# Interleaving two arrays: seven tiles with three shared load buffers in place of eight tiles with four

## The chip, the cores and the metric

The kernel runs on one NeuronCore of a Trainium2 chip. What counts is the device time of one execution in microseconds (us), the median of several runs. A profile was taken of one execution; its span is the time from the first to the last thing that the profiler recorded on that core.

The parts of the core that matter here are 16 DMA engines, which move rows between HBM (the large memory outside the core) and SBUF (128 partitions of memory on the core), VectorE (DVE), which copies inside SBUF, and the two engines that issue DMA transfers, SyncE (SP) and ScalarE (ACT). SP and ACT each have a queue of their own to the 16 DMA engines. Transfers in one queue are taken in order.

## The reference

Two arrays of 32 x 256 x 1024 float32, 33.55 MB each, are woven into one of twice the length: even elements from `x`, odd elements from `y`.

```python
result = np.zeros((batch, seq, dim * 2), dtype=np.float32)
result[..., 0::2] = x
result[..., 1::2] = y
```

No arithmetic is done. 67.1 MB are read and 67.1 MB written.

## The kernel before

`x` and `y` are taken as flat arrays and cut into n = 8 tiles of 128 x 8192 elements: a tile's row on one partition is 8192 elements, 32 KiB, contiguous in HBM. The output of a tile is 128 rows of 16,384 elements. It is made and stored in two halves, h = 0 and h = 1, each 128 x 8192.

There are six SBUF buffers of 32 KiB per partition: `xt` twice and `yt` twice, which tile k uses by k % 2, and `ot` twice, used by half: `ot[0]` always holds the first half of a tile's output and `ot[1]` the second.

Each engine has its own program, and semaphores tie them together:
- **SP** issues the loads. The first half of x(0) comes first (L37), then, in a loop over the tiles, x(k) (L45) and y(k) (L48). From k = 2 on, each load first waits until the tile two before has been copied out of its buffer: the semaphore `woven` counts the copies, four a tile, and the third of tile k-2 is the last that reads its x, the fourth the last that reads its y.
- **ACT** issues the second half of x(0) (L38) and then all stores (L68), two a tile, each after the second copy of its half.
- **VectorE** does four copies a tile, in the order x half 0, y half 0, x half 1, y half 1 (L60 for x, L63 for y). Each writes every second element of `ot[h]`. It waits for the load of x or y at the first half, and before the x copy of each half for the store that had used `ot[h]` in the tile before (`osem[h]`).

At the end ACT waits for the last first-half store, clears the semaphores, and SP waits for the last second-half store. `tile_interleave_kernel` moves the first DMA of SP and the first of ACT to the opening of the program, ahead of a barrier.

In what follows x(k), y(k) are the loads of tile k, and tiles are counted from 0.

Of the kernel before, what the change touches and what calls it, by code (L numbers as in the profile page):

```python
# [3 lines left out]


def _interleave(nc, x, y, out):
    P = 128
    W = 8192
    H = W // 2  # L10

    total = 1
    for s in x.shape:
        total *= s
    n = total // (P * W)
    assert n * P * W == total

    def rows(ap, names, k):
        flat = ap.rearrange("b s d -> (b s d)")
        return flat[k * names : (k + 1) * names].rearrange("(p w) -> p w", p=P)  # L20

    fp32 = mybir.dt.float32
    xt = [nc.alloc_sbuf_tensor(f"xt{b}", [P, W], fp32).ap() for b in (0, 1)]
    yt = [nc.alloc_sbuf_tensor(f"yt{b}", [P, W], fp32).ap() for b in (0, 1)]
    ot = [nc.alloc_sbuf_tensor(f"ot{b}", [P, W], fp32).ap() for b in (0, 1)]

    xsem = [nc.alloc_semaphore(f"xsem{b}") for b in (0, 1)]
    hsem = nc.alloc_semaphore("hsem")
    ysem = [nc.alloc_semaphore(f"ysem{b}") for b in (0, 1)]
    woven = nc.alloc_semaphore("woven")  # L30
    osem = [nc.alloc_semaphore(f"osem{b}") for b in (0, 1)]

    xs = [rows(x, P * W, k) for k in range(n)]
    ys = [rows(y, P * W, k) for k in range(n)]
    os_ = [rows(out, 2 * P * W, k) for k in range(n)]

    nc.sync.dma_start(out=xt[0][:, :H], in_=xs[0][:, :H]).then_inc(xsem[0], 16)  # L37
    nc.scalar.dma_start(out=xt[0][:, H:], in_=xs[0][:, H:]).then_inc(hsem, 16)  # L38

    for k in range(n):  # L40
        b = k % 2
        if k >= 2:
            nc.sync.wait_ge(woven, 4 * (k - 2) + 3)
        if k:
            nc.sync.dma_start(out=xt[b], in_=xs[k]).then_inc(xsem[b], 16)  # L45
        if k >= 2:
            nc.sync.wait_ge(woven, 4 * (k - 2) + 4)
        nc.sync.dma_start(out=yt[b], in_=ys[k]).then_inc(ysem[b], 16)  # L48

    for k in range(n):  # L50
        b = k % 2
        for h in (0, 1):
            c = slice(h * H, (h + 1) * H)
            if h == 0:
                nc.vector.wait_ge(xsem[b], 16 * (k // 2 + 1))
            elif k == 0:
                nc.vector.wait_ge(hsem, 16)
            if k:
                nc.vector.wait_ge(osem[h], 16 * k)
            nc.vector.tensor_copy(out=ot[h][:, 0::2], in_=xt[b][:, c]).then_inc(woven, 1)  # L60
            if h == 0:
                nc.vector.wait_ge(ysem[b], 16 * (k // 2 + 1))
            nc.vector.tensor_copy(out=ot[h][:, 1::2], in_=yt[b][:, c]).then_inc(woven, 1)  # L63

    for k in range(n):
        for h in (0, 1):
            nc.scalar.wait_ge(woven, 4 * k + 2 * h + 2)
            nc.scalar.dma_start(  # L68
                out=os_[k][:, h * W : (h + 1) * W], in_=ot[h]
            ).then_inc(osem[h], 16)  # L70

    nc.scalar.wait_ge(osem[0], 16 * n)
    used = sorted(s.num for s in [*xsem, hsem, *ysem, woven, osem[0]])
    assert used == list(range(used[0], used[-1] + 1)), used
    nc.scalar.sem_clear(range(used[0], used[-1] + 1))
    nc.sync.nop(nofuse=True).wait_op(osem[1], 16 * n, "sem-ge").then_inc(
        osem[1], -16 * n
    )


def kernel(tc, x, y, out):
    nc = tc.nc
    tc.close()
    tc.compile()

    _interleave(nc, x, y, out)

    blocks = nc.main_func.blocks
    for engine in (mybir.EngineType.SP, mybir.EngineType.Activation):
        opening = blocks[0].instructions  # L90
        at, moved = next(
            (b, i)
            for b in blocks[1:]
            for i in b.instructions
            if i.engine == engine and i.opcode == "DMACopy"
        )
        assert not (moved.sync_info and moved.sync_info.on_wait)
        body = at.instructions
        body.remove(moved)
        gate = next(  # L100
            n
            for n, i in enumerate(opening)
            if i.engine == engine and i.opcode == "Drain"
        )
        opening.insert(gate, moved)
        at.instructions = body
        blocks[0].instructions = opening


# [1 line left out]
_INS = ['x', 'y']  # L111
_OUTS = [((32, 256, 2048), 'float32')]


# [23 lines left out]
```

## Time and profile before

| | |
|---|---|
| median of 4 runs | 314.7 us (314.66 to 314.75) |
| the profiled execution | 314.66 us |
| its span | 313.3 us |
| read from and written to HBM | 67.11 MB and 67.11 MB, 428 GB/s over the span |
| x copies (L60), 16 | 36.7 us, 2,295 ns each |
| y copies (L63), 16 | 36.7 us, 2,292 ns each |
| stores (L68), 16 of 4,096 KB | 29.0 us from issue to landing (median) |
| y loads (L48), 8 of 4,096 KB | 60.8 us |
| x loads (L45), 7 of 4,096 KB | 43.7 us |
| halves of x(0) (L37, L38), 2,048 KB each | 11.7 and 13.4 us |

In the lines of the profile, `out_dram<-ot` is a store, `yt<-in_y_dram` a load of y; q1 is the queue of the loads that SP issues and q10 that of ACT. A row of tenths shows the busy share in 40 equal slices of the span. The chain is the path of work that ended last, followed back from the end. The time from issue to landing contains the time a transfer stands behind others in its queue.

### The profile page before, as it was taken

What the parts mean: (1) busy time and instruction counts of PE and PEld (TensorE: products, weight loads), DVE (VectorE), ACT (ScalarE), POOL (GpSimd) and SP (SyncE); (2) the same over time, 40 slices, a digit from 0 to 9 for tenths busy, and PEclk for the clock granted to TensorE, in tenths of its full rate; (3) what the DMA queues carried; (4) which work ended last, traced back from release to release, by engine and by line L of the source; (5) the groups of instructions that cost most, each with busy time, mean ns of one, the idle gap of its engine ahead of it and who ended that gap; (6) DMA issues with size and microseconds to landing.
All of it is one profiled execution on the core that took longest, in us unless ns stands there. A gap on an engine that the chain in (4) does not pass through costs nothing.

```text
span 313.3 us, 113 instructions
## 1 busy us (share of the span) xinstructions
DVE 72.6 (23%) x32; POOL 0.2 (0%) x4
## 2 busy tenths in 40 slices
DVE  0216002232022410324003250031501315013510
POOL 0000000000000000000000000000000000000000
DMA  8999999999999999999999999999999999999997
GB/s 341 462 402 402 452 418 448 422 439 431 422 448 410 460 402 464 406 464 406 464 406 464 406 452 418 448 422 435 435 414 456 410 456 406 464 406 464 406 464 339
DMA packets 4752, 134.22 MB, mean 428 GB/s; under 512 B 528, under 2 KB 528, under 8 KB 528
## 3 DMA queue, kind: packets, MB, share of 16 engines
q10 hardware_dynamic: 2448, 69.21, 51.2%
q1 hardware_dynamic: 2304, 65.01, 48.5%
HBM read 67.11 MB, written 67.11 MB: 428 GB/s over the span
## 4 chain that ended last, share of the span: by engine, by line
DMA 82%; DVE 12%; issue 0%
DMA out_dram<-ot 76%; DMA yt<-in_y_dram 7%; DVE ot L63 6%; DVE ot L60 6%
## 5 line engine op out<-in xcount | busy, mean ns | idle before, releaser
L60 DVE COPY ot<-xt 128x4096 f32<-128x4096 f32 x16 | 36.7, 2295 | 183.0 <-DMA out_dram<-ot 171.2
L63 DVE COPY ot<-yt 128x4096 f32<-128x4096 f32 x16 | 36.7, 2292 | 42.9 <-DMA yt<-in_y_dram 42.9
L122 POOL MEMSET const-bfloat16-1.0<- 128x1 bf16 x1 | 0.1, 101 | 0.0
L122 POOL MEMSET const-uint8-127<- 128x1 uint8 x1 | 0.1, 101 | 0.0
L122 POOL MEMSET const-float32-0.0<- 128x1 f32 x1 | 0.1, 98 | 0.2 <-issue 0.2
L122 POOL MEMSET const-float32-1.0<- 128x1 f32 x1 | 0.1, 98 | 0.0
## 6 DMA issues: line engine op xcount, KB each, us to landing
out_dram<-ot ACTq DMA_DIRECT2D x16, 4096.0 KB, 29.0
yt<-in_y_dram SPq DMA_DIRECT2D x8, 4096.0 KB, 60.8
xt<-in_x_dram SPq DMA_DIRECT2D x7, 4096.0 KB, 43.7
xt<-in_x_dram SPq DMA_DIRECT2D x1, 2048.0 KB, 11.7
xt<-in_x_dram ACTq DMA_DIRECT2D x1, 2048.0 KB, 13.4
```

What stands on the lines that cost most here:

```text
L60: nc.vector.tensor_copy(out=ot[h][:, 0::2], in_=xt[b][:, c]).then_inc(woven, 1)
L63: nc.vector.tensor_copy(out=ot[h][:, 1::2], in_=yt[b][:, c]).then_inc(woven, 1)
L122: nc = _bacc.Bacc("TRN2", target_bir_lowering=False, num_devices=1)
```

## The change

Rows become 36.5 KiB (9,344 elements) in six tiles and 37 KiB (9,472) in a seventh, so n = 7. The four load buffers become three, `lt`, of 37 KiB; the loads are numbered j = 0, 1, 2, ... in the order x(0), y(0), x(1), y(1), ..., and load j uses `lt[j % 3]`. The two output buffers stay half a tile of output, now 37 KiB. Load j waits for the last copy that reads load j-3: y(k+1) for the second x copy of tile k, x(k+2) for the second y copy of tile k. The order of the copies, the waits for the stores, the stores, and the split of the first load between SP and ACT are as they were. The semaphores of x and y become three of the load buffers.

```diff
-    W = 8192
-    H = W // 2
+    W = 9472
+    L = 3
...
+    widths = [9344] * 6 + [W]
...
-    xt = [nc.alloc_sbuf_tensor(f"xt{b}", [P, W], fp32).ap() for b in (0, 1)]
-    yt = [nc.alloc_sbuf_tensor(f"yt{b}", [P, W], fp32).ap() for b in (0, 1)]
+    lt = [nc.alloc_sbuf_tensor(f"lt{b}", [P, W], fp32).ap() for b in range(L)]
     ot = [nc.alloc_sbuf_tensor(f"ot{b}", [P, W], fp32).ap() for b in (0, 1)]
...
+    def load(q, j, c=slice(None)):
+        k, src = j // 2, (x, y)[j % 2]
+        return q.dma_start(
+            out=lt[j % L][:, : widths[k]][:, c], in_=rows(src, 1, k)[:, c]
+        )
...
+    H = widths[0] // 2
+    load(nc.sync, 0, slice(0, H)).then_inc(lsem[0], 16)
+    load(nc.scalar, 0, slice(H, 2 * H)).then_inc(hsem, 16)
+
+    for j in range(1, 2 * n):
+        if j >= L:
+            nc.sync.wait_ge(woven, 4 * ((j - L) // 2) + 3 + (j - L) % 2)
+        load(nc.sync, j).then_inc(lsem[j % L], 16)
...
+        w = widths[k] // 2
+        for h in (0, 1):
+            for i in (0, 1):
+                j = 2 * k + i
+                if h == 0:
+                    nc.vector.wait_ge(lsem[j % L], 16 * (j // L + 1))
+                elif j == 0:
+                    nc.vector.wait_ge(hsem, 16)
+                if k and i == 0:
+                    nc.vector.wait_ge(osem[h], 16 * k)
+                nc.vector.tensor_copy(
+                    out=ot[h][:, i : 2 * w : 2],
+                    in_=lt[j % L][:, h * w : (h + 1) * w],
+                ).then_inc(woven, 1)
...
             nc.scalar.dma_start(
-                out=os_[k][:, h * W : (h + 1) * W], in_=ot[h]
+                out=rows(out, 2, k)[:, h * w : (h + 1) * w], in_=ot[h][:, :w]
             ).then_inc(osem[h], 16)
```

More of the change, by code (lines that the diff above doesn't have):

```diff
@@ L14, in _interleave @@
         total *= s
-    n = total // (P * W)
-    assert n * P * W == total
+    cols = total // P
+    widths = [9344] * 6 + [W]
+    assert cols * P == total and sum(widths) == cols
+    n = len(widths)
+    starts = [sum(widths[:k]) for k in range(n)]
     def rows(ap, names, k):
         flat = ap.rearrange("b s d -> (b s d)")
-        return flat[k * names : (k + 1) * names].rearrange("(p w) -> p w", p=P)
+        a, w = names * P * starts[k], names * widths[k]
+        return flat[a : a + P * w].rearrange("(p w) -> p w", p=P)
@@ L22, in _interleave @@
     fp32 = mybir.dt.float32
-    xt = [nc.alloc_sbuf_tensor(f"xt{b}", [P, W], fp32).ap() for b in (0, 1)]
-    yt = [nc.alloc_sbuf_tensor(f"yt{b}", [P, W], fp32).ap() for b in (0, 1)]
+    lt = [nc.alloc_sbuf_tensor(f"lt{b}", [P, W], fp32).ap() for b in range(L)]
     ot = [nc.alloc_sbuf_tensor(f"ot{b}", [P, W], fp32).ap() for b in (0, 1)]
-    xsem = [nc.alloc_semaphore(f"xsem{b}") for b in (0, 1)]
+    lsem = [nc.alloc_semaphore(f"lsem{b}") for b in range(L)]
     hsem = nc.alloc_semaphore("hsem")
-    ysem = [nc.alloc_semaphore(f"ysem{b}") for b in (0, 1)]
@@ L30, in _interleave @@
     woven = nc.alloc_semaphore("woven")
     osem = [nc.alloc_semaphore(f"osem{b}") for b in (0, 1)]
[L33 to L38, printed above, removed]
-    for k in range(n):
[L41 to L48, printed above, removed]
@@ L50, in _interleave @@
-    for k in range(n):
[L51 to L63, printed above, removed]
@@ L65, in _interleave @@
-    for k in range(n):
+    def load(q, j, c=slice(None)):
[10 more added lines that the diff above has]
+        load(nc.sync, j).then_inc(lsem[j % L], 16)
@@ L66, in _interleave @@
+    for k in range(n):
+        w = widths[k]
         for h in (0, 1):
@@ L68, in _interleave @@
             nc.scalar.dma_start(
-                out=os_[k][:, h * W : (h + 1) * W], in_=ot[h]
+                out=rows(out, 2, k)[:, h * w : (h + 1) * w], in_=ot[h][:, :w]
             ).then_inc(osem[h], 16)
     nc.scalar.wait_ge(osem[0], 16 * n)
-    used = sorted(s.num for s in [*xsem, hsem, *ysem, woven, osem[0]])
+    used = sorted(s.num for s in [*lsem, hsem, woven, osem[0]])
     assert used == list(range(used[0], used[-1] + 1)), used
```

## The prediction

> **What bounds the kernel now.** I read the page first (busy shares, DMA, chain), then the waits, then the busy time by tile, and last the records of the single DMA rows.
>
> ```profile
> DVE 72.6 (23%) x32; POOL 0.2 (0%) x4
> DMA  8999999999999999999999999999999999999997
> DMA packets 4752, 134.22 MB, mean 428 GB/s; under 512 B 528, under 2 KB 528, under 8 KB 528
> q10 hardware_dynamic: 2448, 69.21, 51.2%
> q1 hardware_dynamic: 2304, 65.01, 48.5%
> DMA out_dram<-ot 76%; DMA yt<-in_y_dram 7%; DVE ot L63 6%; DVE ot L60 6%
> ```
>
> The DMA engines are busy in every slice. VectorE is busy for 23% of the span, though 12% of the chain of waits passes through it. Is that 12% time in which the DMA stands still? The view by stretches, cut at the five middle tiles, answers (columns: us, DVE, POOL, PE clock, DMA share, GB/s):
>
> ```profile
> 67.60:106.30 38.70, 9.09 (x4) 0.00 (x0) 1.00 1.00 434
> 106.30:145.10 38.80, 9.09 (x4) 0.00 (x0) 1.00 1.00 432
> 145.10:183.80 38.70, 9.09 (x4) 0.00 (x0) 1.00 1.00 434
> ```
>
> The DMA share is 1.00 in each, so the copies run under transfers. The chain passes through them because it follows semaphores; it doesn't know that another store and a load are under way meanwhile. The waits say the same:
>
> ```profile
> DVE ot L60 <- DMA out_dram<-ot: 171.2, 14, 19.5
> DVE ot L63 <- DMA yt<-in_y_dram: 42.9, 8, 8.0
> SPq L45 <- DVE ot L60: 209.2, 6, 40.8
> ```
>
> SP waits for a buffer, VectorE for a store; nothing here waits for VectorE for lack of speed. The records of single DMA packets give the price. 4,752 packets are 33 transfers x 128 rows, and 33 x 16 packets that only count a semaphore. Of 3,968 rows of 32 KiB, 3,913 took 1,213 ns, loads and stores alike; of 256 rows of 16 KiB, 216 took 611 ns; all 528 semaphore packets (4 bytes) took 9 ns. So 16 KiB costs 602 ns (27.2 GB/s for each of 16 engines) and a packet some 9 ns besides. The first data row starts at 1.01 us, the last ends at 312.97: a window of 311.96 us of which almost nothing is idle. In the middle a tile of four transfers takes 38.72 us (67.64 to 106.36, in the chain), 9.68 each: 8 rows per engine x 1.204 = 9.632, and 0.048 that goes with the transfer and its rows. All 33: 31 x 9.68 + 2 x (4.816 + 0.048) = 309.8 us; some 2.15 us are left for filling and draining.
>
> **The change, part by part.**
>
> *Bytes*: the same 134.22 MB. At one rate, nothing changes.
>
> *Fewer, longer transfers*: 29 in place of 33. Rows are 37,376 B (six tiles) and 37,888 B (one): 1.373 and 1.392 us at 27.2 GB/s. A transfer alone is 8 x 1.373 + 0.048 = 11.03 us, a wide one 11.19; where loads and stores share the engines, 22.07 and 22.37. The sum: 23 x 11.03 + 4 x 11.19 + 2 x 5.54 (the halves of the first x) = 309.6 us, that is 0.2 less (4 transfers x 0.048). By the rows' own prices it would be 32 rows and 4 semaphore packets fewer on each engine, x 9 ns = 0.32; I take 0.2, since the period holds every gap. Not seen is a row of this length. From below: no cost beside the bytes would give 232 x 9 ns = 2.1 us less. From above: the 512 B that a row has beyond 36 KiB cost another packet's 9 ns: 2.1 us more. The three lengths seen (4 B, 16 KiB, 32 KiB) lie on one line, so I take that line.
>
> The 9 ns and 0.048 us stand against the Trainium skill: "DMA: Bandwidth & Descriptors", section on the anatomy of one DMA, gives about 2 us of fixed cost to every transfer, though fitted for the path through GpSimd, which isn't used here. Four transfers fewer would by that save 8 us if it were exposed; the 38.72 us of a tile show that it is hidden behind the next transfer.
>
> *Copies*: 28 in place of 32, each 4,672/4,096 x 2.295 = 2.62 us (the last four 2.65). Off the path as long as another transfer is queued; cover checked below.
>
> *Three shared load buffers*: this is where something could break. Before, x(k+1) and y(k+1) were both in the queue long before tile k was done. Now the load queue holds at most three transfers, and y(k+1) is issued only when the second x copy of tile k is done, x(k+2) after the next copy. SP issues in order, with nothing else behind its waits; an issue takes 0.33 us of SP. Step by step, for the changed kernel:
> - y(0) lands at 1.01 + 1.14 x (22.07 - 1.01) = 25.0 (22.07 is the landing before, 1.14 the ratio of sizes). Its copy ends at 27.6 and the first store is issued; the next two copies (2.52 apart, then 2.62) let y(1) go at 30.1, and x(2) and the second store at 32.7. x(1) alone would last until 23.9 + 11.0 = 34.9, so there is cover.
> - The first store's first row: before, 4.74 us after its issue (24.43 to 29.17), which is the 1.01 of an idle start plus three rows already taken from the loads. Now 1.01 + 3 x 1.38 = 5.2: at 32.8. From then both queues share.
> - x(1) has 6.5 of 8 rows done by then; its end before was 5.47 us later, now 6.3: 39.1. Each load after it ends 22.07 later: y(1) 61.2, x(2) 83.3, ... y(5) 237.7, x(6) 260.1, y(6) 282.5.
> - Stores: the first ends at 32.8 + 1.14 x 17.57 = 52.8, the second at 74.9, landing one turn and 0.36 us later, 76.6 (before: 1.54 later). The x copy ends at 79.2 and y(2) is issued, while x(2) has 4.1 us to go. Both queues advance by 44.14 us a tile, so this picture repeats.
> So the load queue nearly runs dry once a tile, but a store is always queued then (the one issued after y landed, at 65.6, begins at 76.9). Gaps in one queue are filled by the other; only both empty costs time.
>
> The Trainium skill ("Trainium Kernel Development and Optimization", Best Practices) asks for double buffers to overlap DMA and compute, which speaks against three for two streams. By it the two late copies, 5.2 us a tile and some 36 us in all, would stand open; the 1.00 share under 9.09 us of copies in each tile says that the other queue is what matters.
>
> *The end*, where loads are over and only stores are left: two more stores follow y(6), and the last row would end at 312.97 - 0.2 = 312.8. Their start must therefore be seamless at 312.8 - 2 x 11.19 = 290.4. The first of them needs y(6): 282.5 + 1.74 (landing) + 2.65 (copy) = 286.9, and the time from issue to first row. That is 1.01 at least (the idle start), and at most 2.74: before, the same store was issued at 290.26 and began at 293.00, with no gap behind the store ahead of it. So 287.9 to 289.6: cover of 0.8 to 2.5 us. Before it was 0.6 to 2.3 (293.6 less 291.3 to 293.0), so nothing is lost here. The last store is issued 5.3 us after 290.7, under 11.2 us of the other.
>
> *Semaphores*: one fewer to clear, nothing on the path (the last store sets the end).
>
> **Sum**: span 313.3 - 0.2 = 313.1. The profiled execution took 314.66, 1.3 more than its span; the median is 314.70. Forecast 314.5 (its own range 314.1 to 315.0).
>
> **Rivals.**
> 1. *The end opens* (slower). y(2) issued at 79.2 is ready at 80.2 to 81.9. Rows are taken some three ahead: x(2)'s last, which starts at 81.9, at about 77.8, and the next load turn is near 80.5. If the load comes late there, stores take one or two turns and all later loads slip by 1.4 to 2.8 us, once (a later load then has more queue in front). y(6) then ends at 283.9 to 285.3, its store is ready as late as 285.3 + 1.74 + 2.65 + 2.74 = 292.4 in place of 290.4: up to 2.0 idle, 316.5; middle 315.7. It decides from a load end of 283.3 (slow start) or 285.0 (quick start). For it: 0.3 us of slack. Against: the quick start needs two lost turns and more. Chance 0.15.
> 2. *Longer rows are dearer*, or the change doesn't do what it says and a row is cut in two: 464 packets per engine for 264, x 9 ns = 1.8 more, 316.4. For it: no row over 32 KiB in the trace; against: the straight line. 0.07.
> 3. *Rows away from 32 KiB steps run cleaner*: 55 rows took more than 1,213 ns; the mean excess of 3.24 ns x 248 rows is 0.8 us on an engine. All gone: 314.5 - 0.8 = 313.7. Against: the excess lies mostly at the start and where streams meet, which stay. 0.10.
>
> **How the numbers follow.** Forecast 0.68, rivals 0.15, 0.07, 0.10. About 0.2% (0.63 us) is what a measurement here can tell from no change: 314.07 to 315.33 counts as the same. Slower: 0.11 of rival 1, 0.07, and 0.02 of the forecast's spread, 0.20. Faster: 0.09 of rival 3 and 0.02, 0.11. Same 0.69. The range 313.8 to 315.8 leaves out a half of rival 1, rival 2 and the best of rival 3, some 0.18; it cuts off the row bounds of 2.1 us, which would need every row off the line.
>
> **What would show it.** Rows of 1,382 ns (1,401 in the last tile); 44.1 us a tile with DMA share 1.00; copies of 2.62 us; stores that wait only on stores. SP should wait on the copies as now, with x loads landing some 22 us after the one ahead. A hole in the GB/s after the last load, near 288 to 292 us, is rival 1; a row count above 3,712 is rival 2. The forecast is wrong if a middle tile takes other than 44.1, or the last two stores don't touch.

## The result, and the profile after

The changed kernel takes 315.17 us (median of 46 runs, 314.63 to 318.11), the kernel before 314.56 (72 runs, 314.27 to 315.48). The ratio is 1.0023 with a 95% interval of 1.0017 to 1.003: slower by some 0.6 to 0.7 us, where 0.2 us less was forecast. The time lies inside the forecast range of 313.8 to 315.8, on the wrong side of before. That it lies inside is luck: the upper end of the range was set for an opening at the end, and that isn't what happened.

The profiled execution took 315.14 us, its span is 313.8 (before: 314.66 and 313.3). From its page:

```profile
DVE 72.1 (23%) x28; POOL 0.2 (0%) x4
DMA  8999999999999999999999999999999999999997
DMA packets 4176, 134.22 MB, mean 428 GB/s; under 512 B 464, under 2 KB 464, under 8 KB 464
DMA out_dram<-ot 74%; DVE ot L61 12%; DMA lt<-in_y_dram 7%
```

The packets are 3,712 rows and 464 semaphore packets, so no row was cut in two. The view by stretches, one tile to a line (columns: us, DVE, POOL, PE clock, DMA share, GB/s):

```profile
77.29:121.44 44.15, 10.29 (x5) 0.00 (x0) 1.00 1.00 433
121.44:165.58 44.14, 10.28 (x4) 0.00 (x0) 1.00 1.00 434
165.58:209.73 44.15, 10.29 (x5) 0.00 (x0) 1.00 1.00 433
```

A tile takes the 44.14 us of the forecast, with the DMA share at 1.00. In the packet records 2,908 of 2,944 rows of 36.5 KiB took 1,382 ns and all 512 rows of 37 KiB 1,401 ns. The middle is as predicted; the half microsecond is elsewhere. It shows in the same view cut into short slices at the end. The view puts a row into the slice in which it starts, and one row of one engine is a DMA share of 0.15 before and 0.18 after in half a microsecond. Before:

```profile
311.00:311.50 0.50, 0.00 (x0) 0.00 (x0) 1.00 2.27 983
311.50:312.00 0.50, 0.00 (x0) 0.00 (x0) 1.00 0.15 66
312.00:312.50 0.50, 0.00 (x0) 0.00 (x0) 1.00 0.01 0
```

Fifteen engines start their last row in one slice and one in the next. After:

```profile
310.50:311.00 0.50, 0.00 (x0) 0.00 (x0) 1.00 1.05 455
311.00:311.50 0.50, 0.00 (x0) 0.00 (x0) 1.00 1.58 682
311.50:312.00 0.50, 0.00 (x0) 0.00 (x0) 1.00 0.18 76
312.00:312.50 0.50, 0.00 (x0) 0.00 (x0) 1.00 0.18 76
```

One row is 0.175 here. Of the 6 rows in the first slice five are last rows and one is the last but one of an engine that lags (a straggler); 9 engines follow in the second, then one straggler, then the other. By the packet records fourteen engines end between 312.28 and 312.76 us, earlier than in the kernel before for the most part (15 engines from 312.36 to 312.70, one at 312.97); the other two end at 313.13 and 313.42, and the slowest sets the time. The mean of the 16 ends is 312.59, before 312.57. The engines are also out of step in the middle. In slices of about a quarter of a row's time, before:

```profile
100.30:100.60 0.30, 0.00 (x0) 0.00 (x0) 1.00 0.25 109
100.60:100.90 0.30, 0.00 (x0) 0.00 (x0) 1.00 3.03 1311
100.90:101.20 0.30, 0.00 (x0) 0.00 (x0) 1.00 0.76 328
101.20:101.50 0.30, 0.00 (x0) 0.00 (x0) 1.00 0.00 0
```

One row is 0.25 here: 1, 12 and 3 engines start a row, then none until the next turn. After:

```profile
100.00:100.35 0.35, 0.35 (x1) 0.00 (x0) 1.00 0.25 107
100.35:100.70 0.35, 0.35 (x1) 0.00 (x0) 1.00 1.48 641
100.70:101.05 0.35, 0.35 (x1) 0.00 (x0) 1.00 1.97 854
101.05:101.40 0.35, 0.35 (x1) 0.00 (x0) 1.00 0.25 107
```

They are spread over the whole row: 1, 6, 8 and 1. When did they come apart? The semaphore of the first load is raised by its 16 engines within 0.94 us of each other (12.35 to 13.29), against 0.57 before (11.17 to 11.74). Where the first stores join (26 to 33 us), each engine loses some 0.6 to 1 us within its load rows in both kernels. At 40 us two engines of the changed kernel are 0.4 and 0.7 us behind the third last; before, the last was 0.3 us behind. From there on no row is over 0.1 us late.

### The profile page after: what moved, and what is told of

It is laid out like the page before. It is cut to its first block, busy times and chain, and to the rows that moved or that the text cites. A ratio compares the mean times of both kernels' runs of the same rounds, so it can differ in the third digit from the quotient of the medians.

```text
span 313.8 us, 104 instructions
## 1 busy us (share of the span) xinstructions
DVE 72.1 (23%) x28; POOL 0.2 (0%) x4
## 4 chain that ended last, share of the span: by engine, by line
DMA 82%; DVE 12%; issue 0%
DMA out_dram<-ot 74%; DVE ot L61 12%; DMA lt<-in_y_dram 7%
## 5 line engine op out<-in xcount | busy, mean ns | idle before, releaser
L61 DVE COPY ot<-lt 128x4672 f32<-128x4672 f32 (+1 forms) x28 | 72.1, 2598 | 224.5 <-DMA out_dram<-ot 163.8
```

The source lines that it names most:

```text
L61: nc.vector.tensor_copy(out=ot[h][:, i : 2 * w : 2], in_=lt[j % L][:, h * w : (h + 1) * w],).then_inc(woven, 1)
```

## The experiments

Theory 1 was the thin load queue, theory 2 that rows which don't lie on steps of 32 KiB make the engines lose step, theory 3 that longer rows make each disturbance dearer. The first four kernels separate the parts of the change. Ratios are to the kernel before, timed beside each; the diffs are against the kernel named.

**Three shared buffers alone** (against the changed kernel):

```diff
-    W = 9472
+    W = 8192
...
-    widths = [9344] * 6 + [W]
+    widths = [W] * 8
```

> Eight tiles with the rows of before (32 KiB), but the three shared load buffers of the changed kernel: the buffers' part alone. Theory 1 (thin load queue: y(k+1) is issued so late that transfers slip) expects most of the added 0.6 us, a ratio near 1.002 to before, also single runs of 2 us more. Theory 2 (rows that don't start at 32 KiB steps make the 16 DMA engines drift apart) expects the time of before, ratio 1.000 within 0.0005, and a spread of some 0.6 us between the first and the last engine of a load's landing at the start. Theory 3 (a longer row makes each disturbance dearer) expects 1.000 too.

314.54 us, ratio 1.0001 (0.9993 to 1.001). The buffers cost nothing. A tile from the stretches of its profile:

```profile
67.54:106.27 38.73, 9.09 (x4) 0.00 (x0) 1.00 1.00 433
106.27:144.99 38.72, 9.09 (x5) 0.00 (x0) 1.00 1.00 433
```

That is the period before, to 0.01 us, with every load of y issued a tile later. Theory 1 falls, and with it the first rival as a cause of the median.

**Row length alone** (against the changed kernel; four buffers in the same code give the waits of before):

```diff
-    W = 9472
-    L = 3
+    W = 8320
+    L = 4
...
-    widths = [9344] * 6 + [W]
+    widths = [8064, W] * 4
```

> Eight tiles and four load buffers as before, but rows of 31.5 and 32.5 KiB in turn: the row length alone, mean and number of transfers unchanged. Theory 1 (thin load queue) expects the time of before, 1.000. Theory 2 (rows off the 32 KiB steps) expects some 0.6 us more, 1.002, with one or two engines of 16 landing 0.9 us or more behind the first at the start. Theory 3 (longer rows) expects 1.000.

315.42 us, 1.0027 (1.0017 to 1.0037), with a spread of 1.08 us at the first landing. As many transfers and as much data in rows of the same mean length as before cost 0.86 us, so theory 3 falls as well.

Not all of this is lag. In the profile, of the slowest of its runs (315.70 us), the end opens, as in rival 1. The last two stores are issued here:

```profile
292.31 7.33 ACTq L70 DMA_DIRECT2D out_dram<-ot  x2
```

By the packet records 12 of the 16 engines stand idle for 0.08 to 0.62 us, until rows of the first of these stores begin at 293.15 to 293.30. All 16 end late, the first of them too. The slowest engine has no such gap, so the opening doesn't set the time.

**Rows on 4 KiB steps** (against the changed kernel):

```diff
-    W = 9472
+    W = 10240
...
-    widths = [9344] * 6 + [W]
+    widths = [9216] * 6 + [W]
```

> The changed kernel with rows of 36 KiB in six tiles and 40 KiB in the last, in place of 36.5 and 37: every row starts at a 4 KiB step. Theory 1 (thin load queue) expects what the change showed, 1.002, or slightly more for the longer last tile. Theory 2 in the form that 512-byte offsets matter expects 1.000; in the form that anything but 32 KiB steps matters, 1.002. Theory 3 (longer rows) expects 1.002.

314.81 us, 1.0008 (0.9999 to 1.0017): between before and the change, though its last tile has longer rows. Its interval just takes in 1.

**Four deep load buffers with seven tiles**, the output in quarters (against the changed kernel):

```diff
-    L = 3
+    L = 4
+    Q = 4
...
-    ot = [nc.alloc_sbuf_tensor(f"ot{b}", [P, W], fp32).ap() for b in (0, 1)]
+    ot = [nc.alloc_sbuf_tensor(f"ot{b}", [P, 2 * W // Q], fp32).ap() for b in (0, 1)]
...
+        for h in range(Q):
+            m = Q * k + h
...
                     out=ot[m % 2][:, i : 2 * w : 2],
```

> The seven tiles and row lengths of the change with four load buffers, each load issued a tile earlier, paid for by output buffers of a quarter tile: 28 stores of 18.25 KiB rows twice as wide in number (4,672 elements of output per row and piece). Theory 1 (thin load queue) expects the time of before plus 14 more store transfers than the change has, x 0.048 = 0.7 us at most, and no single runs far out; theories 2 and 3 expect 0.6 us above that. With 43 transfers against 33 the bare sum is 0.5 us over before: 1.0015 by theory 1, 1.0035 by theories 2 and 3.

322.71 us, 1.0256 (1.0239 to 1.0273): a miss by 7.0 to 7.7 us for every theory. From the DMA issues of its page:

```profile
out_dram<-ot ACTq DMA_DIRECT2D x24, 2336.0 KB, 20.1
lt<-in_x_dram SPq DMA_DIRECT2D x5, 4672.0 KB, 21.5
```

From its stretches:

```profile
97.50:101.00 3.50, 2.11 (x2) 0.00 (x0) 1.00 1.01 433
101.00:103.50 2.50, 0.55 (x1) 0.00 (x0) 1.00 0.95 404
103.50:106.00 2.50, 1.58 (x2) 0.00 (x0) 1.00 1.03 441
106.00:108.50 2.50, 1.08 (x1) 0.00 (x0) 1.00 0.96 359
```

A store row is now half as long as a load row. The engines take rows of the two queues in turn: the load of x(2) has its rows from 63.21 to 80.54 us, 17.3 us, where 8 x (1.382 + 0.695) = 16.6 and equal bytes would be 22.1. So loads run ahead and run out, and for a time stores alone go through two small buffers.

Idle engines are the smaller part of the loss. The share is 0.99 over the four stretches, and by the packet records an engine is idle for some 1.8 us in all. The rows themselves take 6.9 us an engine beyond the commonest time of a row of their length, against 1.7 in the changed kernel. Most of it comes in bursts where the load queue, empty for a while, joins the stores again: an engine loses 0.4, 1.4, 1.1, 1.4 and 0.7 us there, following the loads issued at 61.1, 105.8, 152.0, 198.8 and 243.8 us. The run says nothing on theories 2 and 3.

The next four put rows of 32 KiB in some places only.

**32 KiB in the first tile** (against the changed kernel):

```diff
-    W = 9472
+    W = 9600
...
-    widths = [9344] * 6 + [W]
+    widths = [8192] + [9472] * 2 + [W] * 4
```

> The changed kernel with rows of 32 KiB in the first tile and 37 and 37.5 KiB in the other six: seven tiles, 29 transfers, three load buffers as in the change; only the rows that start the DMA engines lie on 32 KiB steps. If the engines drift apart while they start (first loads), it takes before less the 0.2 us of four transfers, 314.4 (ratio 0.9995), and the landing of the first load spreads over 0.6 us as in before. If they drift apart where the first stores join, or later, it takes what the change took, 315.2 (1.002).

315.02 us, 1.0017 (1.0008 to 1.0025). The first landing spreads over 0.51 us, as in before; yet one engine loses 0.8 us more than the next one where the first stores join the loads of x(1), now of 37 KiB rows, and it ends 0.77 us behind all others. So the joining matters too. (The "joining" is the moment from which the engines serve stores beside the loads.)

**32 KiB in the first two tiles** (against the changed kernel):

```diff
-    W = 9472
+    W = 9856
...
-    widths = [9344] * 6 + [W]
+    widths = [8192] * 2 + [9728] + [W] * 4
```

> Seven tiles, 29 transfers, three load buffers; 32 KiB rows in the first two tiles, 38 and 38.5 KiB in the other five: the start and the joining of the first stores both run on rows that lie on 32 KiB steps. If start and joining make the engines drift apart and the middle doesn't, 314.4 (ratio 0.9995), less than before; if rows off the steps cost something all along, 315.1 (1.002).

314.30 us, 0.9992 (0.9984 to 1.0001), and in a second set of runs:

> Seven tiles with 32 KiB rows in the first two, once more, to narrow its interval against before: 314.3, a ratio of 0.9993 (0.2 us for four transfers fewer); if the first look was luck, 1.000 or more.

314.22 us, 0.9992 (0.9983 to 1.0001). Rows of 38 and 38.5 KiB in five of seven tiles cost nothing once start and joining are over, and the 0.2 us of four transfers appear. Its engines in the middle and at the end:

```profile
100.35:100.70 0.35, 0.05 (x1) 0.00 (x0) 1.00 0.00 0
100.70:101.05 0.35, 0.00 (x0) 0.00 (x0) 1.00 3.38 1464
101.05:101.40 0.35, 0.00 (x0) 0.00 (x0) 1.00 0.78 338
...
310.50:311.00 0.50, 0.00 (x0) 0.00 (x0) 1.00 2.73 1183
311.00:311.50 0.50, 0.00 (x0) 0.00 (x0) 1.00 0.18 79
```

A row is 0.26 in the first slices and 0.18 in the last: 13 and 3 engines in the middle, 15 and one at the end, so they are in step. Both medians are 0.2 to 0.3 us below before, and both intervals reach just to 1.0001, so a gain is likely but not beyond doubt.

**Off the steps in the first and last tile only** (against the changed kernel):

```diff
-    W = 9472
-    L = 3
+    W = 8320
+    L = 4
...
-    widths = [9344] * 6 + [W]
+    widths = [8064] + [8192] * 6 + [W]
```

> The kernel before (eight tiles, four load buffers) with rows of 31.5 KiB in the first tile, 32 in six, 32.5 in the last: only start and end are off the 32 KiB steps. If the start is where it happens, it takes the 315.4 of the alternating 31.5 and 32.5 KiB rows (1.0025) with a spread of some 1 us between engines at the first landing; if it is the middle or the joining of the first stores, 314.6 (1.000).

315.21 us, 1.0026 (1.0015 to 1.0037), the whole loss from two of eight tiles. The first landing spreads over 0.69 us, less than expected, and the last over 1.49, so most of the drift arises later. In the packet records it is there once the first stores have joined; two rows that start at 26.86 and 26.98 us took 1.2 and 1.4 us more than usual, where the worst row at the joining before took 0.85 more. The stretch around it, here and in the kernel before:

```profile
26.00:36.00 10.00, 2.50 (x2) 0.00 (x0) 1.00 0.94 377
```

```profile
26.00:36.00 10.00, 2.80 (x2) 0.00 (x0) 1.00 1.02 410
```

The difference in share is not the loss: a row counts where it starts, and the extra time of the rows at the joining is the same on the mean, 0.8 us an engine in both. Some engines lose more, others less.

**Rows of 40 KiB** (against the changed kernel):

```diff
-    W = 9472
+    W = 10240
...
-    widths = [9344] * 6 + [W]
+    widths = [4096] + [W] * 6
```

> Seven tiles, three load buffers, rows of 16 KiB in the first tile and 40 KiB in six: all row starts on 8 KiB steps, and the longest rows that fit. If 8 KiB steps are as good as 32 KiB steps, 314.4 (0.9995); if only 32 KiB steps are good, 315.1 (1.002); if the length of a row makes each disturbance dearer (theory 3), 315.3 or more.

314.56 us, 1.0015 (0.9992 to 1.0038); one of 11 runs took 318.89 and widens the interval. By the median, 8 KiB steps are nearly as good as 32, and the longest rows don't hurt. But the half-size first tile also moves the issue of the first store to 13.57 us, so this isn't the step alone.

So is it the steps, or the moment at which the first store meets the loads? The kernels with 32 KiB rows at the start issue it at nearly the same time (24.26 to 24.43 us). Three kernels move it; the first, against the kernel before (the others differ in the number of columns, and the third has the edit in the changed kernel):

```diff
     ot = [nc.alloc_sbuf_tensor(f"ot{b}", [P, W], fp32).ap() for b in (0, 1)]
+    spare = nc.alloc_sbuf_tensor("spare", [P, 1360], fp32).ap()
...
+            if k == 0 and h == 0:
+                nc.vector.tensor_copy(out=spare[:, 0:1360:2], in_=xt[0][:, :680])
```

> The kernel before with one copy of 680 columns more on VectorE ahead of the first y copy (into a spare buffer), so that the first store joins the loads some 0.4 us later; nothing else. If the engines of the DMA lose step because the store happens to arrive at a bad moment against the rows under way (coincidence), the time should move by some tenths of a us, up to 315.2; if what matters is that rows lie on 32 KiB steps, it stays at 314.5 (1.000 within 0.0005).

314.52 us, 1.0003 (0.9995 to 1.0012).

> The same with 1,440 columns, some 0.8 us later; a row of 32 KiB takes 1.21, so the three moments (0, 0.4, 0.8) cover a row. Coincidence: at least one of the two off 314.5 by 0.3 us or more. Steps of 32 KiB: 314.5.

314.71 us, 1.0009 (1.0 to 1.0018).

> The changed kernel with the first store joining some 0.7 us (half a row) later, by a copy of 1,250 columns into a spare buffer. Coincidence: the time moves, down to 314.4 if the moment becomes good. Steps of 32 KiB: 315.2 as before the edit.

315.12 us, 1.0021 (1.0012 to 1.003). The copies moved less than was meant: the first store is issued at 24.77 and 25.04 us in place of 24.43, and its first row starts at 29.04 and 29.08 in place of 29.17, since the engines take it at their next turn. In the second, nine engines take it at 29.08 to 29.45 and seven a row later, at 30.60 to 31.02, and the time rises by 0.2 to 0.3. In the changed kernel the issue moves from 27.71 to 28.21 and the first row from 31.57 to 32.99, a whole row, and the time stays. There three engines had taken it at 31.57 to 31.73 and 13 from 32.99 on; now nine take it at 32.99 to 33.66 and seven from 34.70 on. So the moment has some part. No kernel brought all 16 engines of the changed kernel to take the first store in the same turn, so that the moment is the cause is not ruled out.

Last, whether the place of the row starts or the length of the rows does it. Three kernels leave work out, as their expectations say; they have four or five runs each. The first, against the kernel before:

```diff
-    H = W // 2
+    U = 8064
+    H = U // 2
...
-        return flat[k * names : (k + 1) * names].rearrange("(p w) -> p w", p=P)
+        whole = flat[k * names : (k + 1) * names].rearrange("(p w) -> p w", p=P)
+        return whole[:, : U * (names // (P * W))]
...
-            nc.sync.dma_start(out=xt[b], in_=xs[k]).then_inc(xsem[b], 16)
+            nc.sync.dma_start(out=xt[b][:, :U], in_=xs[k]).then_inc(xsem[b], 16)
```

> The kernel before with every row cut to 31.5 KiB while the row starts stay on 32 KiB steps: 1/64 of the output is left out (the last 128 elements of each row of x and y). The bare sum is 309.8/64 = 4.84 us less, 309.7. If the place of the row starts is what matters, 309.7 and 16 engines within 0.6 us at the end; if rows of other than 32 KiB length are enough, 310.5 (as with 31.5 KiB rows packed without gaps, 0.9 us over before).

Four runs of 309.37, 309.55, 310.31 and 310.32 us, median 309.93. Its profile (309.37) has the engines within 0.32 us at the end.

> The kernel before with rows of 32 KiB that start 32.5 KiB apart in x and y (65 in the output), seven tiles: it leaves out the last 128 elements of each row and what lies behind the seventh tile, 1/8 of the bytes in all. Seven periods of 38.72 us in place of eight: 314.5 - 38.7 = 275.8. If the place of the row starts is what makes the engines lose step, 276.4 or more, and in the profile landings of the loads spread over 1.2 us or more in the middle; if the length of the rows is, 275.8 and a spread of 0.6.

Its edit sets U = 8192, takes tiles 8,320 apart and n = 7. Five runs of 275.75, 275.80, 275.95, 276.15 and 276.62 us, median 275.95; the profile is of the last, with a spread of 1.39 us.

> The kernel before with rows cut to 30 KiB that still start 32 KiB apart (64 in the output, the second half of each output row at 30): 1/16 of the output is left out. Bare sum 309.8/16 = 19.4 us less: 295.2. If the place of the row starts matters, 295.2 and a spread of 0.6 us; if the length does, 295.8 or more.

Its edit is U = 7680. Four runs from 295.14 to 295.63, median 295.40; spread 0.32 us in the profile of 295.14. The three medians lie 0.15 to 0.25 us above the good case, which is an estimate from the bare sum, and single runs on both sides of it; two of the four runs at 31.5 KiB come near the bad case (310.5), and one of the five at 32.5 KiB apart reaches it (276.4). Neither place nor length alone brings the 0.6 us each time; this stays open.

Across the 13 profiles of the whole computation with half-tile stores, the time goes with the spread of the 16 engines at the last store's landing:

```
kernel                           last landing spread, us   that execution, us
two tiles of 32 KiB              0.42                      314.28
before, store 0.4 later          0.45                      314.38
three buffers, 32 KiB            0.56                      314.54
40 KiB rows                      0.56                      314.52
before                           0.62                      314.66
two tiles of 32 KiB, again       0.72                      314.71
before, store 0.8 later          0.75                      314.71
36 KiB rows                      0.93                      314.99
31.5 and 32.5 KiB in turn        1.07                      315.70
one tile of 32 KiB               1.10                      314.95
the change                       1.11                      315.14
the change, store 0.7 later      1.43                      315.45
off the steps in tile 0 and 7    1.49                      315.45
```

In twelve of them the first of the 16 engines lands between 312.49 and 312.71 us, so nearly all the difference is the spread. With 31.5 and 32.5 KiB in turn it lands at 313.27: that is the kernel whose end opened.

The packet records show one thing more that goes with the spread. In the kernels with up to 0.72 us all 16 engines begin the first store in the same turn, except in the one with 40 KiB rows (11 engines, then 5). In the seven from 0.75 us up they are split over two turns: 3 and 13 in the change and with 36 KiB rows, 12 and 4 with 31.5 and 32.5 KiB in turn, 13 and 3 with tiles 0 and 7 off the steps, 15 and 1 with one tile of 32 KiB, 9 and 7 in the two kernels with a later store. This is not shown to be the cause. The 40 KiB rows are split without the loss; of the shortened kernels, the one with 30 KiB rows is split (2 and 14) and has a spread of 0.32 us, and the one with 32.5 KiB steps isn't and has 1.39.

## Why the prediction was wrong

**What held.** The two row times, the period, the copies (2.60 us measured, 2.62 predicted) and the packet count came out as priced; y(0) landed at 25.06 (25.0 predicted). Behind the joining the loads were 0.7 to 1 us later than predicted: y(2) was issued at 79.91 (79.2), y(6) landed at 285.2 (284.2). The load queue does nearly run dry, and it costs nothing: y(2) is issued at 79.91 while the rows of x(2) last until 84.53, and after 35 us no row takes over 0.1 us more than usual. The last two stores touch (289.91 to 302.23 and 301.10 to 313.42 us over all engines), and no engine is idle near 290 us, so the end doesn't open in the profiled run. The three-buffer run says the same of the median. The rule on double buffers (the Trainium skill, "Trainium Kernel Development and Optimization", Best Practices) was rightly set aside here: three buffers for two streams measured 1.0001.

**The saving of 0.2 us** for four transfers is real as far as it could be seen: the two medians of seven tiles with an even start are 0.2 and 0.3 us below before.

**The step that failed** is the sum "All 33: 31 x 9.68 + 2 x (4.816 + 0.048) = 309.8 us; some 2.15 us are left for filling and draining": the 2.15 us were carried to the changed kernel as a constant. After, the window from the first row (0.99) to the end of the last (313.42) is 312.43 us; less the predicted 309.6 that leaves 2.83. The 0.68 us more, less the saving of 0.2, is the 0.5 us of the span. Some 0.4 of the 0.68 is lag: the slowest engine ends 0.83 us behind the mean of the 16, before 0.40. The rest is the mean engine's: it ends at 312.59, before 312.57, where 0.2 less was forecast. Filling is not one number but 16: each engine loses its own share while the first loads run and when the first stores join, nothing later lets it catch up, and the time is that of the slowest. The sum was made for one mean engine; the window was that of the slowest.

**The joining had no price.** The prediction says "Gaps in one queue are filled by the other; only both empty costs time." The four-buffer run shows otherwise: a queue that comes back costs each engine 0.4 to 1.4 us. In the changed kernel it costs this once, 0.9 us on the mean (0.8 before). The first store's first row was put at 5.2 us after its issue, by "three rows already taken from the loads". Three engines began it after 3.9 to 4.0 us, the other 13 after 5.3 to 6.4: the step fits most engines and misses that they part there.

**Rival 3 pointed the wrong way.** It took the excess of 55 rows over 1,213 ns as something that rows away from 32 KiB steps might shed. The changed kernel has more: counting half rows and whole rows by their means, 16 x 38 + 248 x 3.2 ns = 1.4 us an engine before, and 16 x 52 + 184 x 4.9 = 1.7 after. With "the excess lies mostly at the start and where streams meet" it had the right places, and a possible loss there was given no bound. The chance of "slower" was put on other mechanisms.

**Rivals 1 and 2.** No row was cut. Four of the 46 runs took 317.0 to 318.1 us, more than any of the 72 runs before and more than a spread of 1 to 1.5 us gives. Whether the end opened in these isn't known, since none was profiled; the three-buffer kernel on 32 KiB rows had none above 315.1 in 11 runs, the one with 40 KiB rows had one of 318.89.

**What stays open** is why rows packed at other than 32 KiB spread the engines at the start. Shown is that start and joining are the place (32 KiB rows in the first two tiles take the loss away, other rows in the first and last tile alone bring it), and that neither buffer sharing nor the longer row does it. Not separated are the place of the row starts, the length of the rows, and whether the first store reaches all 16 engines in the same turn.

## What to carry to other kernels

Where DMA is busy from end to end, a sum over bytes gives the mean engine; the time is that of the slowest of 16, so look at the spread of a transfer's 16 landings, first and last, before trusting a few tenths of a microsecond. Shapes chosen for the middle should not set the start: here the first two tiles decided, and the other five could have rows of 38 and 38.5 KiB. And be wary of rows of very unequal length on two competing queues: in the one kernel here that had them at two to one, the queue with the longer rows ran empty, and every time it joined again cost each engine 0.4 to 1.4 us.

## What the runs showed of the hardware

- Two queues on one DMA engine are served row by row, not byte by byte: with 36.5 KiB load rows against 18.25 KiB store rows a load took 17.3 us in place of 22.1. The Trainium skill ("DMA: Bandwidth & Descriptors", section on queues, rings and completion order) has the engines take packets of the queues in turn; in the traces here the packet is a whole row, up to 40 KiB.
- When the store queue joins the loads, an engine loses 0.7 to 1.2 us on the mean in the kernels of the table, mostly in one or two load rows that start some 1 to 6 us after the issue (in the kernel before 25.92 to 27.76, with the issue at 24.43). The first row of the first store begins 3.9 to 4.8 us after its issue in these kernels, on some engines a row later than on others.
- It costs the same kind of loss when a load queue that ran empty joins the stores: 0.4 to 1.4 us an engine, five times in the kernel with four load buffers.
- An engine keeps its lag: in the changed kernel two engines are 0.4 and 0.7 us behind the third last at 40 us and 0.37 and 0.66 us behind it at the end, 270 us later.
- The skill's advice on row starts (same page, section on latency and other measured facts) is to pad away from large powers of two, measured there from 512 KiB apart. At 32 KiB apart no kernel here gained that left the power of two from the first tile on; whole rows packed at 31.5, 32.5 and 36.5 KiB lost 0.6 to 0.9 us.
